# Twelve small loads, two groups of six, in SP's queue of a rotary-embedding kernel

## The chip, the cores and the metric

The kernel runs on one core of a Trainium2 chip. The metric is the device time of one execution in microseconds; lower is better. Three runs of the kernel before took 162.36, 162.38 and 162.53 us, median 162.38.

## The reference, cut to what matters

```python
x = x.reshape(batch, seq, num_heads, head_dim)          # 16, 512, 16, 64; float32
x1, x2 = x[..., :half_dim], x[..., half_dim:]
cos = cos[None, :, None, :]
sin = sin[None, :, None, :]
rotated = np.concatenate([x1 * cos - x2 * sin, x1 * sin + x2 * cos], axis=-1)
```

Each head's 64 numbers are two halves of 32, which are rotated by an angle that depends on the position in the sequence. 33.5 MB are read and 33.5 MB are written; every number of x is used for two products.

## The kernel before, in words

The batch is cut into eight tiles (`NT`) of two sequences each. A tile has 128 partitions, 64 for each sequence, and 8192 numbers in a partition: 8 rows (`R`) of 1024, 32 KB, so a tile is 4096 KB. Five buffers in SBUF (`NB`, line 73) take the eight tiles: tiles 0 to 4 get a buffer each, and tiles 5, 6 and 7 reuse those of tiles 0, 1 and 2. The result is written over the input in its buffer and stored from there.

A tile's work is cut into groups of two or three rows (`GROUPS`), and `PLAN` gives the order of the operations of each tile. `T` on POOL multiplies the swapped halves by the signed sine (line 144), `P` on DVE multiplies by the cosine (147), and `S` on DVE adds the two (149). For some groups `B` does the sine's product on DVE, or `A` and `M` do the cosine's on DVE (151) and the sum on PE (156, 158), which ACT copies back (159). The order on every engine is the one in which the program is written (`manual_schedule`, line 65).

All loads and stores of x are issued by SP, in the order of the program, and SP waits at each of them until its conditions hold; nothing behind it is issued meanwhile. ACT issues the two loads of the tables (88, 89). SP's order is: tile 0 in four pieces, tile 1 in two, tiles 2, 3, 4 (lines 86 to 93), then store 0, store 1, store 2 (179), loads 5, 6, 7 (181), stores 3 and 4 (183), and stores 5, 6 and 7 (186), the last in three pieces.

What a DMA waits for: a store waits for the tile's last computation; a load into a used buffer waits for the store that empties it. Besides, eight completion semaphores serve all DMAs of SP and ACT, in turn, in the order of the program. Each DMA takes the next one, and waits until the DMA that had it eight places earlier has landed. In the kernel before, the places are these (semaphore: DMAs in order):

| semaphore | DMAs |
|---|---|
| 0 | x0 piece 1, x2, load 7 |
| 1 | sine, x3, store 3 |
| 2 | cosine, x4, store 4 |
| 3 | x0 piece 2, store 0, store 5 |
| 4 | x0 piece 3, store 1, store 6 |
| 5 | x0 piece 4, store 2, store 7 piece 1 |
| 6 | x1 piece 1, load 5, store 7 piece 2 |
| 7 | x1 piece 2, load 6, store 7 piece 3 |

Of the kernel before, what the change touches and what calls it, by code (L numbers as in the profile page):

```python
# [7 lines left out]
FP32 = mybir.dt.float32  # L8
# [4 lines left out]
def kernel(  # L13
# [8 lines left out]
    nc = tc.nc  # L22
# [28 lines left out]
    xv = x.rearrange("b (p r) d -> (b p) (r d)", r=R)  # L51
    xv = xv.rearrange("(t p) f -> t p f", p=P)
# [5 lines left out]
    fixed = ctx.enter_context(tc.tile_pool(name="fixed", bufs=1))  # L58
# [19 lines left out]
    def load(t, *cuts):  # L78
        for a, b in cuts or ((0, R),):
            loads[t].append(nc.sync.dma_start(out=x_tiles[t][:, a * dim:b * dim], in_=xv[t][:, a * dim:b * dim]))  # L80

    def store(t, *cuts):
        for a, b in cuts or ((0, R),):
            stores[t].append(nc.sync.dma_start(out=ov[t][:, a * dim:b * dim], in_=x_tiles[t][:, a * dim:b * dim]))
# [7 lines left out]
    for t in range(2, NB):  # L92
        load(t)

    ident = fixed.tile([P, P], FP32, name="ident")
    nc.gpsimd.memset(ident, 0.0)  # L96
    nc.gpsimd.affine_select(  # L97
        out=ident, in_=ident, compare_op=ALU.not_equal, fill=1.0,
# [5 lines left out]
                          in_=bass.AP(tensor=i64.tensor, offset=i64.offset, ap=[i64.ap[0], [0, BP], [1, HP]]))  # L104
# [74 lines left out]
            store(t)  # L179
    for t in range(NB, NT):  # L180
        load(t)
    for t in range(NT - NB, NB):
        store(t)
    for t in range(NB, NT):
# [37 lines left out]
```

## Time and profile before

| | |
|---|---|
| median of 3 runs | 162.38 us |
| the profiled execution's own time | 162.55 us |
| its span | 160.8 us |
| DVE busy, POOL busy | 138.4 us (86%), 130.3 us (81%) |
| PE busy, ACT busy | 58.5 us (36%), 14.1 us (9%) |
| moved by DMA | 67.25 MB, mean 418 GB/s |

All rows of the prediction come from that one execution. A DMA is told by two times: when its instruction stood on SP, and how long after that it landed, which is when its semaphore reached the full count. Together they give:

| DMA | issued, us | to landing, us | landed, us |
|---|---|---|---|
| x0 piece 1 (first) | 0.74 | 3.9 | 4.6 |
| x0 piece 4 | 2.11 | 11.7 | 13.8 |
| x1 piece 2 | 3.19 | 20.4 | 23.6 |
| x2 | 4.95 | 28.3 | 33.2 |
| x3 | 5.32 | 37.7 | 43.0 |
| x4 | 6.56 | 46.6 | 53.2 |
| store 0 | 30.06 | 32.8 | 62.9 |
| store 1 | 56.82 | 15.8 | 72.6 |
| store 2 | 66.12 | 16.3 | 82.4 |
| load 5 | 66.55 | 25.5 | 92.05 |
| load 6 | 72.66 | 29.1 | 101.8 |
| load 7 | 82.44 | 29.0 | 111.4 |
| store 3 | 82.87 | 38.3 | 121.2 |
| store 4 | 109.06 | 21.8 | 130.9 |
| store 5 | 119.76 | 20.8 | 140.6 |
| store 6 | 131.69 | 18.5 | 150.2 |
| store 7 piece 1 | 138.51 | 15.3 | 153.8 |
| store 7 piece 2 | 143.2 | 13.1 | 156.3 |
| store 7 piece 3 | 150.09 | 9.9 | 160.0 |

(x2's 28.3 is worked out: the profile gives 33.0 as the median of x2 and x3 together.)

In the page's slices each digit is the busy share of a fortieth of the span in tenths, 9 for nine tenths and more. In the list of DMA queues a row has the queue, its packets, the megabytes, and the time of its packets as a share of what 16 engines could give; q1 is SP's queue, q10 ACT's, q14 fetches of instructions. A row of a waits list has who waited for whom, the microseconds in total, how often, and the longest.

### The profile page before, as it was taken

Reading aid. Unit: us, or ns where it says so; the run is one execution under the profiler, and the core shown is the slowest. Engines: PE = TensorE matmul, PEld = TensorE weight load, DVE = VectorE, ACT = ScalarE, POOL = GpSimd, SP = SyncE. Lnnn points to the kernel's source line nnn. Section 1 sums busy time; section 2 is a strip of 40 time slices with the busy share of each in tenths; the row PEclk is TensorE's granted clock in tenths of the full one; section 3 lists DMA queues with packets and bytes.
Section 4 is the critical chain, followed back from the end, with each engine's and each line's share of the span. In section 5 each row is a group of like instructions: output and inputs, shape, how many; then the busy total and the mean of one; then the engine's idle time right before and its main releaser. Section 6 shows DMA issues by size and latency. Waiting matters only on the chain.

```text
span 160.8 us, 394 instructions
## 1 busy us (share of the span) xinstructions
PE 58.5 (36%) x84; PEld 18.3 (11%) x84; DVE 138.4 (86%) x48; ACT 14.1 (9%) x25; POOL 130.3 (81%) x29
## 2 busy tenths in 40 slices
PE   0500000130488803088702378896868620000000
PEld 0200000100122100032101022222222200000000
DVE  0069999999999999999999999999998999999300
ACT  3200000000011110011200011102121210000000
POOL 2299999999979299995999199999999999992000
PEclk9999999999999995557995555559999995555555
DMA  5999999999999999999999999999999999999994
GB/s 164 384 450 417 460 432 465 391 432 481 391 391 505 399 399 489 416 399 481 424 399 448 457 399 432 473 391 432 473 399 424 467 408 416 465 424 408 404 441 199
DMA packets 3329, 67.25 MB, mean 418 GB/s; under 512 B 384, under 2 KB 512, under 8 KB 768
## 3 DMA queue, kind: packets, MB, share of 16 engines
q1 hardware_dynamic: 3168, 67.11, 97.8%
q10 hardware_dynamic: 160, 0.13, 0.2%
q14 instruction: 1, 0.01, 0.0%
HBM read 33.69 MB, written 33.55 MB: 418 GB/s over the span
## 4 chain that ended last, share of the span: by engine, by line
DVE 37%; POOL 27%; DMA 18%; PE 7%; issue 2%; ACT 2%; DVEq 0%; POOLq 0%
POOL T L144 27%; DVE x_sb L149 18%; DVE pp L147 16%; DMA x_sb<-in_x_dram 16%; PE ps L158 3%; PE ps L156 3%; DMA tabs<-in_sin_dram 3%; DVE x_sb L151 1%; DVE T L144 1%; ACT x_sb L159 1%; PE pp L111 1%; ACT sns L116 0%; ACT sns L117 0%; DVEq L149 0%; POOLq L144 0%
## 5 line engine op out<-in xcount | busy, mean ns | idle before, releaser
L144 POOL TENSOR_TENSOR T<-x_sb,sns 128x3072 f32<-128x3072 f32 (+1 forms) x22 | 129.3, 5927 | 14.7 <-ACT sns L117 5.4
L147 DVE TENSOR_TENSOR pp<-x_sb,tab 128x3072 f32<-128x3072 f32 (+1 forms) x20 | 60.8, 3040 | 8.8 <-ACT tab L117 8.3
L149 DVE TENSOR_TENSOR x_sb<-T,pp 128x3072 f32<-128x3072 f32 (+1 forms) x20 | 60.7, 3033 | 2.9 <-POOL T L144 1.5
L156 PE MATMUL ps<-T,ident 128*128 128x512 f32 x40 | 30.5, 854 | 47.1 <-POOL T L144 27.7
L158 PE MATMUL ps<-x_sb,ident 128*128 128x512 f32 x40 | 28.6, 807 | 18.9 <-DVE x_sb L151 18.9
L159 ACT COPY x_sb<-ps 128x512 f32<-128x512 f32 x20 | 11.7, 586 | 110.4 <-PE ps L158 110.4
L156 PEld LDWEIGHTS ps<-T,ident 128*128 128x128 f32 x40 | 7.6, 237 | 69.8 <-POOL T L144 29.2
L158 PEld LDWEIGHTS ps<-x_sb,ident 128*128 128x128 f32 x40 | 9.7, 252 | 34.8 <-DVE x_sb L151 23.3
L151 DVE TENSOR_TENSOR x_sb<-x_sb,tab 128x2048 f32<-128x2048 f32 x5 | 11.4, 2281 | 0.0
L144 DVE TENSOR_TENSOR T<-x_sb,tab 128x2048 f32<-128x2048 f32 x3 | 6.8, 2280 | 0.0
L111 PE MATMUL pp<-tabs,sel 64*128 64x256 f32 x2 | 1.2, 697 | 5.1 <-DMA tabs<-in_sin_dram 5.1
L116 ACT ACT_TABLE_LOAD x1 | 1.3, 1283 | 1.9 <-issue 1.9
L111 PE MATMUL tab<-tabs,sel 64*128 64x256 f32 x2 | 1.2, 708 | 0.3 <-DMA tabs<-in_cos_dram 0.3
L111 PEld LDWEIGHTS pp<-tabs,sel 64*128 64x128 f32 x2 | 0.5, 310 | 5.0 <-issue 5.0
L116 ACT COPY sns<-pp 128x256 f32<-128x256 f32 x1 | 0.4, 373 | 3.1 <-PE pp L111 3.1
L111 PEld LDWEIGHTS tab<-tabs,sel 64*128 64x128 f32 x2 | 0.5, 310 | 1.0 <-DMA tabs<-in_cos_dram 1.0
L96 POOL MEMSET ident<- 128x128 f32 x1 | 0.2, 205 | 0.3 <-POOLq L203 0.3
L117 ACT ACTIVATE sns<-pp 128x256 f32<-128x256 f32 x1 | 0.4, 390 | 0.0
L97 POOL TENSOR_SCALAR_AFFINE_SELECT ident<-ident 128x128 f32<-128x128 f32 x1 | 0.3, 292 | 0.1
L103 POOL COPY sel<-ident 64x128 f32<-64x128 f32 x1 | 0.3, 283 | 0.1
L203 POOL MEMSET const-float32-0.0<- 128x1 f32 x1 | 0.1, 98 | 0.2 <-issue 0.2
L116 ACT COPY tab<-pp 128x64 f32<-128x64 f32 x1 | 0.2, 197 | 0.9 <-PE tab L111 0.9
(4 smaller groups left out, 0.5 us busy)
## 6 DMA issues: line engine op xcount, KB each, us to landing
out_dram<-x_sb SPq DMA_DIRECT2D x7, 4096.0 KB, 20.8
x_sb<-in_x_dram SPq DMA_DIRECT2D x6, 4096.0 KB, 29.1
out_dram<-x_sb SPq DMA_DIRECT2D x2, 1536.0 KB, 12.6
x_sb<-in_x_dram SPq DMA_DIRECT2D x1, 2560.0 KB, 20.4
x_sb<-in_x_dram SPq DMA_DIRECT2D x1, 2048.0 KB, 11.7
x_sb<-in_x_dram SPq DMA_DIRECT2D x1, 1536.0 KB, 14.8
x_sb<-in_x_dram SPq DMA_DIRECT2D x2, 512.0 KB, 4.5
x_sb<-in_x_dram SPq DMA_DIRECT2D x1, 1024.0 KB, 7.3
```

Of the source, the lines that this page charges most:

```text
L97: nc.gpsimd.affine_select(out=ident, in_=ident, compare_op=ALU.not_equal, fill=1.0, base=0, pattern=[[-1, P]], channel_multiplier=1,)
L103: nc.gpsimd.tensor_copy(out=sel.rearrange("k (b p) -> k b p", b=BP), in_=bass.AP(tensor=i64.tensor, offset=i64.offset, ap=[i64.ap[0], [0, ...
L111: spread = [nc.tensor.matmul(out=o.rearrange("p r j -> p (r j)"), lhsT=sel, rhs=tabs[:, i], start=True, stop=True) for i, o in ((1, sin_ps ...
L116: signed.append(nc.scalar.copy(out=o[:, :, 1, :], in_=sin_ps[:, r0:r0 + o.shape[1], :]))
L117: signed.append(nc.scalar.mul(out=o[:, :, 0, :], in_=sin_ps[:, r0:r0 + o.shape[1], :], mul=-1.0))
L144: return [eng.tensor_tensor(out=Ts[t, k], in0=swapped(xr, n), in1=tb, op=ALU.mult)]
L147: return [nc.vector.tensor_tensor(out=pps[t, k], in0=xr, in1=cosb(k), op=ALU.mult)]
L149: return [nc.vector.tensor_tensor(out=xr, in0=Ts[t, k], in1=pps[t, k], op=ALU.add)]
L151: return [nc.vector.tensor_tensor(out=xr, in0=xr, in1=cosb(k), op=ALU.mult)]
L156: made.append(nc.tensor.matmul(out=ps, lhsT=ident, rhs=Ts[t, k][:, c * C:(c + 1) * C], start=True, stop=False))
L158: made.append(nc.tensor.matmul(out=ps, lhsT=ident, rhs=xc, start=False, stop=True))
L159: made.append(nc.scalar.copy(out=xc, in_=ps))
```

## The change

A tile `marks` of 16 partitions is added. Twelve loads write pieces of it: load i of n partitions reads the first 16 + n numbers of the first n partitions of x's tile 0 (68 bytes for one partition to 124 for fifteen) and writes them into columns of their own. Nothing reads the tile. The first six have 3, 6, 8, 11, 14 and 15 partitions and stand behind the load of tile 4, the second six have 1, 2, 4, 7, 10 and 13 and stand behind load 7. All are issued by SP; together they have 94 rows.

```diff
     for t in range(2, NB):
         load(t)
+
+
+    marks = fixed.tile([16, 12 * 32], FP32, name="marks")
+
+    def mark(i, n):
+        nc.sync.dma_start(out=marks[:n, 32 * i:32 * i + 16 + n], in_=xv[0][:n, :16 + n])
+
+    for i, n in enumerate((3, 6, 8, 11, 14, 15)):
+        mark(i, n)
 
     ident = fixed.tile([P, P], FP32, name="ident")
...
     for t in range(NB, NT):
         load(t)
+    for i, n in enumerate((1, 2, 4, 7, 10, 13)):
+        mark(6 + i, n)
     for t in range(NT - NB, NB):
         store(t)
```

The order on PE, DVE, ACT and POOL is unchanged. The twelve loads take their turns at the eight semaphores, so the places of all later DMAs move. As built (small loads m0 to m11):

| semaphore | DMAs |
|---|---|
| 0 | x0 piece 1, x2, m5, m7, store 6 |
| 1 | sine, x3, store 0, m8, store 7 piece 1 |
| 2 | cosine, x4, store 1, m9, store 7 piece 2 |
| 3 | x0 piece 2, m0, store 2, m10, store 7 piece 3 |
| 4 | x0 piece 3, m1, load 5, m11 |
| 5 | x0 piece 4, m2, load 6, store 3 |
| 6 | x1 piece 1, m3, load 7, store 4 |
| 7 | x1 piece 2, m4, m6, store 5 |

## The prediction

> **What bounds the kernel now.** I read the page's slices (part 2) first, then the DMA queues (part 3), then every DMA issue with its time to landing, and last the waits of SP's queue.
>
> ```profile
> DMA  5999999999999999999999999999999999999994
> GB/s 164 384 450 417 460 432 465 391 432 481 391 391 505 399 399 489 416 399 481 424 399 448 457 399 432 473 391 432 473 399 424 467 408 416 465 424 408 404 441 199
> ...
> q1 hardware_dynamic: 3168, 67.11, 97.8%
> ```
>
> Queue q1, SP's, keeps 16 engines busy for 97.8% of the 160.8 us span, and no slice between the first and the last falls under 9 tenths. DVE (86%) and POOL (81%) leave more room. The chain of waits is spread over POOL, DVE and DMA, which misleads here: it takes whichever release came last, while the stream of transfers never stops.
>
> The landings prove that. Landing is issue plus time to landing. From x4 on, the tiles land at 53.2, 62.9, 72.6, 82.4, 92.05, 101.8, 111.4, 121.2, 130.9, 140.6 and 150.2 us: x4, store 0, 1, 2, load 5, 6, 7, store 3, 4, 5, 6. That is issue order, a tile every 9.7 us (4.19 MB / 9.7 us = 432 GB/s), whatever the kind. A later issue therefore costs nothing as long as the transfer ahead of it is still running. Some issues from SP's timeline, and their landings from the DMA issues of the same stretch:
>
> ```profile
> 30.06 0.35 SPq L84 DMA_DIRECT2D out_dram<-x_sb  x1
> ...
> 56.82 0.34 SPq L84 DMA_DIRECT2D out_dram<-x_sb  x1
> ...
> 109.06 0.34 SPq L84 DMA_DIRECT2D out_dram<-x_sb  x1
> ...
> 150.09 0.33 SPq L84 DMA_DIRECT2D out_dram<-x_sb  x1
> ```
>
> ```profile
> out_dram<-x_sb SPq DMA_DIRECT2D x1, 4096.0 KB, 32.8
> ...
> out_dram<-x_sb SPq DMA_DIRECT2D x1, 4096.0 KB, 15.8
> ...
> out_dram<-x_sb SPq DMA_DIRECT2D x1, 4096.0 KB, 21.8
> ...
> out_dram<-x_sb SPq DMA_DIRECT2D x1, 1536.0 KB, 9.9
> ```
>
> The first store is issued at 30.06 us and lands at 62.9, so it stood 23 us behind x2, x3 and x4. I call the time from an issue to the landing of the transfer ahead of it its **lead**. Store 1 has 62.9 - 56.82 = 6.1 us, store 2 has 6.5, store 4 has 121.2 - 109.06 = 12.1, and the last piece 6.2 (156.3 - 150.09). A lead must cover the time from issue to first bytes. The very first load bounds that: 0.5 MB issued at 0.74 lands 3.9 us later, of which 1.2 us is transfer at 432 GB/s, so 2.7 us. Every lead exceeds it; there is no hole in the stream.
>
> **The change part by part.** It removes nothing and moves nothing on PE, DVE, ACT or POOL: their order stands. On SP it adds twelve issues, and because the eight completion semaphores go round in turn, it changes which earlier DMA each later one must wait for.
>
> *SP's own time.* The present loads take SP 0.33 to 0.81 us to issue, 0.43 in the median (x_sb's instructions on SP); twelve are 5 us. SP's waits cover them:
>
> ```profile
> SPq L84 <- DVE x_sb L149: 91.6, 9, 16.4
> SPq L84 <- ACT x_sb L159: 24.7, 3, 11.0
> SPq L80 <- DMA out_dram<-x_sb: 14.6, 2, 9.4
> ```
>
> SP sits idle 91.6 us for DVE alone. Cost 0.
>
> *First six, behind x4.* Their waits are x0's last three pieces, x1's two and x2, which land by 33.2 us. SP stands there until then, with store 0 queued behind it. Store 0 now takes the semaphore of x3, which lands at 43.0 (5.32 + 37.7). So it is issued at 43.0 and not 30.06, and its lead falls from 23.1 to 53.2 - 43.0 = 10.2 us: above 2.7, cost 0. Store 1 waits for x4 (53.2), before its data are ready at 56.82: no change. Store 2 waits for the first small load, which follows x4 in the stream, at about 53.3; it is issued at 66.12 anyway. Loads 5 to 7 wait for small loads long landed, and, as now, for the stores that free their buffers.
>
> *Second six, behind load 7.* Load 7 is issued at 82.44. Five of the small loads follow at once. The sixth takes load 5's semaphore and holds SP until 92.05. Store 3 then takes load 6's: issued at 101.8 in place of 82.87, lead 111.4 - 101.8 = 9.6 us. Store 4 takes load 7's: 111.4 in place of 109.06, lead 9.8. Store 5 and later ones wait for small loads that land just after load 7, before their data are ready (store 5 at 119.76). No lead is under 6.1 us. Cost 0. If this cover were gone, each store issued too late would stop the stream for up to 2.7 us.
>
> *The bytes and packets themselves.* These do stand in the stream. No row shows a packet of 68 to 124 bytes, so I bound it. In a 10 ns window at 3.96 us the queue of the tables has one completion packet of few bytes:
>
> ```profile
> q10 hardware_dynamic: 1, 0.00, 5.6%
> ```
>
> That is 0.056 x 16 x 10 ns = 9 ns. Above lies a table row of 1 KB: in the first 8 us q10 takes 5.0% of 16 x 8 us = 6.4 us for 128 rows and 32 completions, so (6400 - 32 x 9) / 128 = 48 ns. By size between them, a row of about 100 bytes is 9 + 39 x 100/1024 = 13 ns. The 64-row and 128-row loads spread their rows evenly, four and eight for each completion packet, so I let a load of up to 15 rows put one on an engine, and let the unluckiest engine be in all twelve: 12 x (13 + 9) = **0.26 us**. At the ends, 12 x (9 + 9) = 0.22 and 12 x (48 + 9) = 0.68. Were all 94 rows to fall on one engine, it would be 94 x 13 + 12 x 9 ns = 1.3 us, or 4.6 at 48 ns. I take 0.26, by the row of nearest size.
>
> *What of this reaches the end.* The span ends with the slowest of the 16 engines, and they don't end together. The GB/s of 158 to 160 us, in slices of 50 ns, count packets by their start; the last packets are 12 KB each, so 246 is one:
>
> ```profile
> GB/s 492 737 492 246 737 0 492 492 246 246 492 0 246 246 0 0 246 0 0 0 0 246 246 0 0 0 0 0 0 0 0 0 0 0 0 0 0 0 0 0
> ```
>
> The last two engines begin their last packet at 159.05 to 159.15, one at 158.8, and all others by 158.7. They spread earlier too. In the same view of 51.5 to 53.5 us one packet of 32 KB stands alone at 52.85, the others of its round begin by 52.3:
>
> ```profile
> GB/s 0 0 0 0 0 0 0 655 1966 1311 0 1966 656 1311 1311 655 0 0 0 0 0 0 0 0 0 0 0 655 0 0 0 0 2621 655 655 1966 655 1311 655 1311
> ```
>  An engine that is 0.35 us ahead of the last swallows 0.26 us of small packets. Only if the loaded engine is one of the two late ones does its share come through. So: twelve loads, 0.26 us on the worst engine, between 0 and 0.26 at the end. The 1.75 us around the span (162.55 - 160.8) stays. The sum is 162.55 + 0 to 0.26. I take +0.1, so 162.65 against the profiled execution. This lies 0.17 above the median 162.38, so **162.5** for the median.
>
> **The rivals.** A measurement of this kernel tells about 0.2%, 0.32 us, from no change.
>
> *Small packets are dear (slower, chance 0.20).* If a small row costs its engine 50 to 100 ns, or rows bunch on few engines, an engine is held 0.7 to 1.3 us, of which up to 0.4 is swallowed: about 163.0 to 163.7, I say 163.2. For it: no such row is in the trace. Against it: packets of few bytes take 9 ns. The Trainium skill speaks for this one: "DMA: Bandwidth & Descriptors", section "Specifications", says that transfers under 512 bytes make the DMA engine read, modify and write. No run here shows such a data row.
>
> *Completions in a row block (slower, chance 0.14).* Each of six small loads ends in a completion with almost no data between. If an engine holds what follows until the completion has landed, it pays the way there: the last engine has passed x4's completion when it starts on store 0 at 52.85, and x4's landing is 53.2, so 0.3 us. Twelve make 3.6, less up to 0.4 of slack: 165.8. The place is behind x4 and load 7; it decides from about two such holds on. Against it: a hold would also show at every boundary of big transfers. Store 6 to the 1.5 MB piece behind it is 153.8 - 150.2 = 3.6 us, a tile of 4 MB is 9.7; 2.44 us a MB leaves no fixed part. The Trainium skill, same page, section "Queues, rings and completion order", calls the increment a strongly ordered write that lands only behind all earlier writes of its engine; the boundaries show that such a write does not stop data behind it, but not six in a row.
>
> *A late store empties the queue (slower, chance 0.05).* Store 0, 3 or 4 would need a lead under its start-up. One hole costs up to 2.7 us, so 163 to 165; leads of 9.6 us and more speak against.
>
> *An engine loses its lag (faster, chance 0.07).* What held one engine half a microsecond near 52 us stands in no row that I read. If SP's longer program moves it to an engine that is ahead, the end comes up to 0.4 us earlier: 162.0. For it speaks only that the lag belongs to one engine.
>
> *The change does not do what it says*: the built order has all twelve small loads on SP, so this has no chance of its own.
>
> **How the numbers follow.** The forecast has 0.54, dear packets 0.20, blocking 0.14, an empty queue 0.05, a lost lag 0.07. Slower by over 0.2% is 0.20 + 0.14 + 0.05 = 0.39, same 0.54, faster 0.07. The likeliest case's own range is 162.3 to 162.7. For 8 in 10 it must take in the dear packets with their upper bounds, up to 164.2, and go a little below to 162.2; blocking stays out.
>
> **What would show it.** In the changed profile: store 0 issued at about 43.0, store 3 at 101.8, store 4 at 111.4, landings still 9.7 us apart, no slice of the DMA row under 9, and about 94 + 94 packets more on q1 if each small row brings its own completion. I am wrong if two landings around 53 or 111 us stand more than 10 us apart (dear or blocking packets), or if the stream has a hole ahead of a store (leads). If the spread of the last packets changes and nothing else, it was the engines' lag.

## The result and the profile after

| | before | after |
|---|---|---|
| median | 162.43 us (7 runs, 162.36 to 162.62) | 162.99 us (7 runs, 162.78 to 163.33) |
| the profiled execution, its span | 162.55 us, 160.8 us | 163.21 us, 161.4 us |
| last landing | 160.0 us | 160.3 us |
| span left after it | 0.8 us | 1.1 us |

The ratio is 1.0036, 95% interval [1.0025, 1.0048]: 0.58 us slower. That is more than the 0.2% that tells a change from none, and above what the forecast's sum could give; it lies inside the stated range.

The slices and queues of the page after:

```profile
DMA  5999999999999999999999999999999999999993
GB/s 159 387 453 411 453 452 447 390 455 455 390 447 456 398 414 463 422 414 463 422 414 463 414 414 471 414 414 439 447 406 455 432 414 455 430 414 409 412 435 164
DMA packets 3517, 67.26 MB, mean 417 GB/s; under 512 B 572, under 2 KB 700, under 8 KB 956
...
q1 hardware_dynamic: 3356, 67.12, 97.6%
```

No slice between the first and the last has fallen under 9: there is no hole. The tiles land in issue order, by their semaphores' last updates: x4 at 52.90 us, store 0 at 62.74, load 7 at 111.52, store 3 at 121.39, and no two tiles in a row, from x4 to store 6, more than 9.95 us apart. The prediction's sign of being wrong, two landings over 10 us apart, did not come. Before, the page counted 3329 packets. The 188 more are 94 rows and 94 completions, so every row went to an engine of its own with a completion of its own. The Trainium skill, "DMA: Bandwidth & Descriptors", section "Why a DMA increments its semaphore by 16 and not by 1", lets a load of n rows use the largest number of engines up to 16 that divides n; the count agrees.

The issues of store 0, store 3, store 4 and the last piece, from SP's timeline after:

```profile
43.25 0.38 SPq L84 DMA_DIRECT2D out_dram<-x_sb  x1
...
101.88 0.37 SPq L84 DMA_DIRECT2D out_dram<-x_sb  x1
...
111.59 0.37 SPq L84 DMA_DIRECT2D out_dram<-x_sb  x1
...
150.21 0.33 SPq L84 DMA_DIRECT2D out_dram<-x_sb  x1
```

These are the predicted 43.0, 101.8 and 111.4. The stores became late as worked out, and the last piece was issued 0.12 us later than before. SP's waits show where the rest went; each row has the total, the number of waits and the longest:

```profile
SPq L84 <- DVE x_sb L158: 41.2, 6, 11.5
SPq L84 <- DMA x_sb<-in_x_dram: 37.3, 4, 9.4
SPq L99 <- DMA x_sb<-in_x_dram: 32.4, 6, 9.4
...
SPq L228 <- DMA out_dram<-x_sb: 9.8, 1, 9.8
```

The second row is the late stores, which wait for loads to land, and the third the small loads; in their place the first fell from 91.6 to 41.2. SP's idle time changed its owner. The last row is the end of the program, where SP waits for all semaphores. Before, it had this form:

```profile
SPq L217 <- DMA out_dram<-x_sb: 9.3, 3, 3.6
```

Three waits of at most 3.6 us, one for each piece of store 7 as it landed, had become a single one of 9.8 us. As built, SP waits at the end for semaphores 3, then 4 and 2, 5 and 1, 6 and 0, and last 7, in five wait instructions. Before, the last piece stood on 7, so everything else had been waited for when it landed. After the change it stands on 3, the first: SP sleeps through all landings, and four more wait instructions come after the last one. The wait ends at 150.21 + 0.33 + 9.8 = 160.3 us, and 1.1 us of the span are left, against 0.8 before. The first instruction behind these waits is a DRAIN; its rows, before and after, give the first and the last start of three:

```profile
L217 SPq DRAIN  x3: 7/7/7, 160.0 to 160.3; - x3
```

```profile
L228 SPq DRAIN  x3: 7/7/7, 160.7 to 161.0; - x3
```

In the trace's finer times it starts 0.08 us after the last landing before the change (159.95, 160.03) and 0.33 us after (160.35, 160.68), with the four wait instructions some 60 ns apart between.

So the span's longer time has two parts: the last landing is 0.40 us later, and the end takes 0.25 us longer. (These are two single executions, 0.65 us apart; the medians differ by 0.56.)

The GB/s of 158 to 160 us after, in slices of 50 ns as in the prediction:

```profile
GB/s 0 492 737 492 492 246 492 246 737 0 492 246 983 0 0 492 246 246 0 492 0 246 0 0 0 0 0 0 246 0 246 0 0 0 0 0 0 0 0 0
```

The last two engines begin their last packet at 159.4 and 159.5, where it was 159.05 to 159.15; the others do so by 159.05, where it was 158.8. In these two executions the whole group ended later, not one unlucky engine.

### The profile page after: what moved, and what is told of

Its sections match the earlier page's. It is cut to its first block, busy times and chain, and to the rows that moved or that the text cites. A ratio compares the mean times of both kernels' runs of the same rounds, so it can differ in the third digit from the quotient of the medians.

```text
span 161.4 us, 407 instructions
## 1 busy us (share of the span) xinstructions
PE 58.4 (36%) x84; PEld 18.3 (11%) x84; DVE 138.4 (86%) x48; ACT 14.0 (9%) x25; POOL 130.2 (81%) x29
## 4 chain that ended last, share of the span: by engine, by line
DVE 36%; POOL 27%; DMA 18%; PE 7%; issue 2%; ACT 2%; DVEq 0%; POOLq 0%
POOL T L153 27%; DVE x_sb L158 18%; DVE pp L156 16%; DMA x_sb<-in_x_dram 16%; PE ps L167 3%; PE ps L165 3%; DMA tabs<-in_sin_dram 3%; DVE x_sb L160 1%; DVE T L153 1%; ACT x_sb L168 1%; PE pp L120 1%; ACT sns L125 0%; ACT sns L126 0%; DVEq L158 0%; POOLq L153 0%
```

## The experiments

The turn theory: the end costs 0.25 us because the last piece has moved to the semaphore that SP waits for first, and the rest is packets in the stream. Its rivals: all of it is packets (rows or packet theory), or all of it comes of the stores' later issue (late-stores theory). After the first four runs a fourth was added: small loads in a burst cost more than the sum of their packets (burst theory).

Each was timed against the kernel before on the same chip, in five rounds. "Full round" means that the number of added loads is a multiple of eight, so that the pieces of store 7 stand on semaphores 5, 6 and 7, as before.

**The end put right, the rest kept.**

```diff
     for t in range(NT - NB, NB):
         store(t)
+    for i in range(12, 16):
+        mark(i, 1)
```

> The changed kernel with four more loads of one row between store 4 and store 5. That moves the last three pieces of store 7 from semaphores 1, 2, 3 back to 5, 6, 7, where they were before the change, and keeps all twelve small loads and all late stores. Turn theory: SP waits for the semaphores at the end in the order 3, 4, 5, 6, 7; with the last piece on 3 four more wait instructions follow its landing, about 0.25 us, which go away here; the rest, 0.3 us, is rows and stays: ratio to the kernel before 1.002. Rows theory (all 0.56 us is packets in the stream): 1.0036 to 1.004. Late-stores theory: 1.0036.

Measured 1.0015, [1.0004, 1.0027]. SP's waits at the end are three again:

```profile
SPq L230 <- DMA out_dram<-x_sb: 9.6, 3, 3.6
```

The turn theory's 1.002 holds; 1.0036 lies outside the interval.

**The end alone.** The kernel before with only these four single rows.

> The kernel before with four loads of one row between store 4 and store 5 and nothing else: the last piece of store 7 comes to stand on semaphore 3. No store is held later than its data, and four rows are at most four times 22 to 35 ns on one engine. Turn theory: 0.25 us slower, ratio 1.0015. Rows theory: 1.0000 to 1.0005. Late-stores theory: 1.0000.

Measured 1.0016, [1.0005, 1.0026], 0.26 us. The stream ended no later than before, and the single long wait is there:

```profile
SPq L226 <- DMA out_dram<-x_sb: 9.3, 1, 9.3
```

The last piece is issued at 150.20, the wait ends at 150.20 + 0.33 + 9.3 = 159.8 us, and 1.1 us of its span of 160.9 are left. Four rows of 68 bytes cost 0.26 us by the place at which they leave the semaphores. Rows theory, at 1.0005 at most, lies at the interval's lower end; together with the run above and the instructions behind the last landing, the turn is shown.

**The same 94 rows in eight loads.**

```diff
-    for i, n in enumerate((3, 6, 8, 11, 14, 15)):
+    for i, n in enumerate((15, 15, 15, 12)):
...
-    for i, n in enumerate((1, 2, 4, 7, 10, 13)):
+    for i, n in enumerate((10, 10, 10, 7)):
```

> The same 94 rows in eight loads in place of twelve: 15, 15, 15 and 12 behind x4, 10, 10, 10 and 7 behind load 7. Eight is a full round of the semaphores, so the pieces of store 7 stand where they stood, and store 0 is not held for x3. Turn theory: only rows are left, ratio 1.001 to 1.002. Rows theory (all of it packets): 1.0036. Late-stores theory: 1.0000.

Measured 1.0006, [0.9993, 1.0020]. The same rows and completions cost less in bursts of four loads than in bursts of six, by the middle of the intervals; they overlap, and the traces below decide it.

**A store with no lead.** Seven loads of one row behind x4 and one behind load 7.

> Seven loads of one row behind x4 and one behind load 7: a full round, so the end is as before, and hardly any rows; but store 0 takes x4's semaphore and is issued only when x4 has landed, so its lead is 0 and the stream runs empty. This measures what a late store costs once its lead is gone. All theories agree that it costs something; the lead argument of the prediction says up to 2.7 us, ratio 1.01 to 1.017. If the stream makes up for the hole later: 1.000.

Measured 1.0193, [1.0173, 1.0213], 3.1 us. Store 0 is issued as x4 lands:

```profile
52.85 0.38 SPq L84 DMA_DIRECT2D out_dram<-x_sb  x1
```

The GB/s of 52 to 54 us in slices of 50 ns show the empty stream:

```profile
GB/s 0 0 0 0 0 0 0 0 0 0 0 0 0 0 0 0 0 0 0 0 0 0 0 0 0 0 0 0 0 0 0 0 0 0 4588 1966 3277 655 0 0
```

The first packets of store 0 begin at 53.7, 0.85 us after its issue, and it lands 11.2 us after it; a tile in a full stream takes 9.7. By this estimate a lead of about 1.5 us would have sufficed where the prediction asked for 2.7; no run tried one between 0 and 6 us. Loads 6 and 7 wait for stores 1 and 2:

```profile
73.81 0.34 SPq L80 DMA_DIRECT2D x_sb<-in_x_dram  x1
...
84.45 0.33 SPq L80 DMA_DIRECT2D x_sb<-in_x_dram  x1
```

Before, they were issued at 72.66 and 82.44, so they are 1.15 and 2.0 us late. The empty stream itself cost 1.1 us: store 0 lands at 64.0 and not 62.9. About 2 us more were lost behind it, where no store is held. The trace's packets say where: the last packets of store 2, begun at 81.7 to 81.9, take 1.66 to 2.31 us on the 16 engines, and those of load 7, begun at 111.8 to 112.5, take 1.60 to 1.89, where such a packet takes 1.21. Each costs 0.9 us, and store 4 lost a further 0.3. The two stand where the stream turns between stores and loads; why they were slow stays open. None of the delay was won back.

**Fifteen rows in every small load**, with the four single rows that restore the end.

```diff
-    for i, n in enumerate((3, 6, 8, 11, 14, 15)):
+    for i, n in enumerate((15, 15, 15, 15, 15, 15)):
...
-    for i, n in enumerate((1, 2, 4, 7, 10, 13)):
+    for i, n in enumerate((15, 15, 15, 15, 15, 15)):
```

> As the run with four more single-row loads, but each of the twelve small loads has fifteen rows: fifteen engines get twelve rows each, and no engine that is ahead can hide the others' delay; stores as late as in the changed kernel, end as before the change. Packet theory (13 + 9 ns for a row and its completion): 0.26 us on nearly every engine, all of it at the end, ratio 1.0016. Burst theory (an engine that has passed more than about four small loads in a row loses another 0.15 to 0.4 us on the large transfer behind them): 0.26 + 0.3 to 0.8 us, ratio 1.0035 to 1.0065. Late-stores theory: as the run with four more loads, 1.0015.

Measured 1.0056, [1.0044, 1.0068], 0.91 us: burst theory. At the prediction's prices the packets give 0.26 us of it.

**One row in every small load**, in the same places, with the same late stores.

> The same sixteen loads in the same places, each of one row. If single rows go to one and the same engine, it alone bears everything. All waits and late issues of stores are those of the changed kernel. Late-stores theory: the cost of the changed kernel less its end, ratio 1.0015 or more. Packet theory: up to 0.35 us on one engine, hidden unless it is one of the last: 1.000 to 1.001. Burst theory: up to 0.8 us on one engine, less its lead over the last: 1.000 to 1.003, and the middle of the 16 engines unmoved in the trace.

Measured 0.9997, [0.9988, 1.0006]. Its stores are as late as those of the changed kernel, and the span of its profiled execution, the fastest of its twelve, is 160.5 us. From its timeline:

```profile
42.82 0.38 SPq L84 DMA_DIRECT2D out_dram<-x_sb  x1
...
101.28 0.37 SPq L84 DMA_DIRECT2D out_dram<-x_sb  x1
...
111.00 0.37 SPq L84 DMA_DIRECT2D out_dram<-x_sb  x1
```

Late stores with a lead cost nothing, twelve issues on SP cost nothing, and delays that meet one engine alone stay hidden behind the last ones. The last of these was the prediction's picture; the change, with rows on up to fifteen engines, isn't that case.

**Small rows by themselves.** Eight loads of 128 rows, 64 bytes each.

```diff
-        nc.sync.dma_start(out=marks[:n, 32 * i:32 * i + 16 + n], in_=xv[0][:n, :16 + n])
+        nc.sync.dma_start(out=marks[:, 16 * i:16 * (i + 1)], in_=xv[0][:, :16])
```

> Eight loads (four behind x4, four behind load 7), each of 128 rows of 64 bytes: 64 rows and 8 completions on every engine, no store held, end as before the change. This prices a small row by itself. Packet theory: 64 x 12 + 8 x 9 ns = 0.84 us, ratio 1.005. If a row costs 30 to 35 ns, as the whole of the changed kernel's shift would give: 2 us, 1.0125. If rows under 512 bytes cost a read, a change and a write each: over 1.0125.

Measured 1.0049, [1.0030, 1.0069], 0.80 us for 64 rows and 8 completions on every engine: 11 ns a packet.

**Rows of 512 bytes.** Four such loads and four single rows.

> Four loads of 128 rows of 512 bytes and four of one row of 64 bytes, in pairs, in the same places: 32 rows of 512 bytes on every engine. By bytes and packets (512 bytes at 27 bytes a ns, and 8 ns for the packet): 32 x 27 ns = 0.87 us, ratio 1.005. If a small row is dear for being under 512 bytes, this run costs less for each row than the 64-byte rows; if it isn't, it costs more, by the bytes.

Measured 1.0065, [1.0049, 1.0081], 1.05 us for 32 rows, 33 ns each. A row of 512 bytes costs more than one of 64. The Trainium skill, "DMA: Bandwidth & Descriptors", section "Specifications", puts transfers under 512 bytes through a read, a change and a write; whatever the engine does, these runs show no price for it.

**Bursts of six with rows between the completions.** As the fifteen-row run, with 128 rows of 64 bytes in each of the twelve.

> Six loads behind x4 and six behind load 7 as in the fifteen-row run, but each of 128 rows of 64 bytes, so that eight rows (about 100 ns) stand between two completions on every engine; the four single rows that restore the end stay. By packets, priced by the eight-load run of 64-byte rows (0.79 us for eight loads, 0.1 us a load): 1.2 us, ratio 1.0073. If the burst's cost comes from the number of small loads in a row, the fifteen-row run's surplus of about 0.25 us a burst comes on top: 1.7 us, 1.0105. If it comes from completions too close together, the rows between them hide it: 1.0073 or less.

Measured 1.0054, [1.0035, 1.0074]. So 1.0105 lies outside: rows between the completions take some of the surplus away, though this run moves 1536 small rows where the fifteen-row run moves 180 and costs as much. How much is left, the traces below show.

**Five in a row.** Five loads of fifteen rows behind x4, three behind load 7.

> Five loads of fifteen rows behind x4 and three behind load 7: a full round, no store held, end as before. With four in a row (94 rows in eight loads) the trace's stream moved by some 50 ns at x4, with six of fifteen rows by 350 to 390. If the surplus starts with the fifth load in a row: about 200 ns at x4 and 40 to 50 at load 7, ratio 1.0015. If it starts with the sixth: 80 and 40 ns, ratio 1.0005 to 1.001. Packet theory alone: 8 x 22 ns, 1.001.

Measured 1.0008, [0.9995, 1.0021]; the time alone doesn't choose. The traces do. For each run I took, from its trace's packets, the mean time at which a tile's 128 packets end, less that of the kernel before, and how much this grows from x4 to store 0 and from load 7 to store 3. That is a mean over 16 engines; times 16 and divided by the engines that a load reaches (one for each row, at most 16; 57/4 and 37/4 in the second row of the table) it is the delay of an engine that takes part in every load. The run with four single rows has no small load at these two places and gives -39 and 7 ns, so a growth of some 40 ns is not told from none. The last column is steadier: by how much the first two packets of store 0 or store 3 on each engine took longer than the usual 1213 ns, mean of 16 engines. In the kernel before it is 5 and 6.

| loads in a burst, rows each | mean growth, ns | per engine in all of them, ns | packets behind held, ns |
|---|---|---|---|
| 3 of 15 | 38 | 41 | 5 |
| 4, some 15 to 7 | 46 and 42 | 52 and 73 | 42 and 20 |
| 5 of 15 | 165 | 176 | 155 |
| 6 of 15 | 375 and 315 | 400 and 336 | 319 and 285 |
| 6 of 1 | 29 and 36 | too small to multiply | 20 and 21, all on one engine |
| 4 of 128 (64 bytes) | 265 and 261 | 265 and 261 | 6 and 3 |
| 6 of 128 (64 bytes) | 490 and 490 | 490 and 490 | 175 and 145 |
| 2 of 128 (512 bytes), 2 of 1 | 356 and 394 | not one number | 12 and 14 |
| the change, 6 and 6 | 116 and 80 | not one number | 127 and 32 |

Up to four loads cost 13 to 18 ns each, less than the 22 of the prediction, and hardly hold what follows. The fifth adds over 100 ns and the sixth over 150.

The packets of the fifteen-row run show where. Behind x4 the small rows run through, one with its completion every 15 ns, and the first packet of store 0 takes its usual 1.21 us on all but one engine (1.27). Its second packet takes 1.35 to 1.79 us on fifteen engines and 1.21 on the one without small rows. In the run of single rows one engine's second packet takes 1.50 us behind x4 and 1.45 behind load 7, all others 1.25 or less: that engine loses some 0.3 us to each burst, which stays hidden. In the changed kernel itself eight engines' second packets take 1.37 to 1.61 us behind x4, and two engines' 1.32 and 1.52 behind load 7; the run with its end put right has eight and two as well.

With eight rows between completions six loads still hold the packets behind them by 145 to 175 ns, now the first and the second, where four such loads hold them by 3 to 6. So both count: how many small loads stand in a row, and how closely they follow; the rows between them take away about half. Every small load has one completion on an engine, so no run tells whether the completion or another part of a load does it. In the GB/s of 52 to 56 us (slices of 100 ns) the hold can be seen: first four in a row, then six of fifteen rows, then six with rows between:

```profile
GB/s 1988 1656 991 0 0 0 0 0 0 0 0 655 1638 1966 983 0 0 0 0 0 0 0 0 328 1638 1638 1311 328 0 0 0 0 0 0 0 328 1311 1311 1966 0
```

```profile
GB/s 672 1360 1980 4 667 0 0 6 329 0 0 328 655 1311 1966 0 655 0 0 0 328 0 0 328 0 0 0 655 0 2294 655 655 0 328 0 655 0 0 0 655
```

```profile
GB/s 36 68 99 765 1727 1366 1008 660 0 0 0 0 0 0 0 0 655 1311 2294 983 0 0 0 0 0 0 0 0 328 0 1638 2294 983 0 0 0 0 0 0 0
```

With four, the 16 engines begin their packets of store 0 as one group every 1.2 us. With six, the group that begins together at 53.1 to 53.6 has come apart a packet later, from 54.7 to 55.5: some engines were held longer than others. With rows between, the group stays together. What in the engine causes the hold was not found.

## Why the prediction was right and wrong

- **What bounds the kernel: right.** The stream of transfers does, and nothing made up for the hole in it: its 1.1 us were never won back, and more was lost behind it. The price of a store without a lead, "up to 2.7 us", was passed: 3.1 in all.
- **SP's time and the late stores, cost 0: right.** The issues came at 43.25, 101.88 and 111.59, and the single-row run shows that all of it together is free. The bound of 2.7 us on the lead was safe; 1.5 is the estimate from the empty stream.
- **A small packet, 13 ns, and a completion, 9 ns: right.** In the trace after the change the rows take 12 or 13 ns and nearly all completions 9; by the times it is 11 ns a packet in the run with 512 such packets a burst, and less than 22 ns for a load in short bursts.
- **"The sum is 162.55 + 0 to 0.26": a term is missing.** The 1.75 us around the span did stay (163.21 - 161.4 = 1.8), but the end of the span, behind the last landing, grew from 0.8 to 1.1. The prediction followed the semaphores' places for every store, and said of the later ones "Cost 0"; it did not follow them to the wait at the end of the program, where their order decides how many waits follow the last landing. That term is 0.25 us, nearly half of the result, and it would be there with four loads of one row.
- **"What of this reaches the end", between 0 and 0.26 us: too small.** The packet price held, but six small loads in a row cost an engine 0.34 to 0.40 us a burst and not 0.13. Over the two bursts the engines that take part in most loads lose more than the slack of 0.35 us can swallow. The stream's part came out at 0.24 us (the run with its end put right) to 0.30 (0.56 less the 0.26 of the end). 162.99 lies outside the likeliest case's own 162.3 to 162.7 and inside the stated range only because that was drawn up to 164.2 for another rival, dear packets; as far as these two causes go, that was luck.
- **The rival "Completions in a row block": half right.** It had the place (behind x4 and load 7), and something behind a burst is held. It put the price at 0.3 us for each of twelve; measured are 13 to 18 ns for each of the first four and 0.1 to 0.2 us for the fifth and the sixth. That the hold is a wait for the completion's landing, as it supposed, is not shown.
- **"Small packets are dear": refuted** by rows of 64 bytes, 7 to 16 ns each by the ends of the interval. **"A late store empties the queue": refuted** by the leads, which stayed; the run without a lead shows what it would have cost. **"An engine loses its lag": did not come.** The last two engines' completions of the last piece land 0.56 us behind the fourteenth's (159.78, then 160.34 and 160.35), so the lag was there after the change too.

## What to carry to other kernels

Adding a DMA anywhere shifts which semaphore every later DMA takes: follow the new places through the waits of later DMAs, and also into the waits at the end, where the DMA that lands last should be waited for last (0.25 us here). In a kernel bound by one stream of transfers a late issue was free with leads of 6 us and more and dear with none; some 1.5 us should do by the estimate above. What enters the stream is paid by the engine that gets it, so ask how many engines share the delay and how far the last one is behind. Don't put more than four tiny loads in a row into such a stream where most engines take part in all of them.

## What the runs showed of the hardware that was not expected

- Five and more tiny loads in a row hold an engine: it loses 52 to 73 ns to four loads, 176 to five, 336 to 400 to six of fifteen rows. Most of the loss is not among the small packets but in the second 32 KB packet behind them, with six 1.33 to 1.79 us in place of 1.21. With eight rows of 64 bytes between completions about half of it is left.
- An empty stream costs 0.85 us from a store's issue to its first packets, 1.5 us by its landing.
- After the hole behind x4, another 2 us were lost in that run, most of it in the last packets of store 2 and of load 7, which took up to 2.31 us; why stays open.
